# Three gemms of a two-block network take their product in token form, and the mixed value is turned by transposes

## Chip, cores and metric

The kernel runs on one core of a Trainium2 chip. The metric is the device time of one execution in microseconds, as the median of the runs. Engines: PE (TensorE, the matrix engine, with PEld for its weight loads), DVE (VectorE), ACT (ScalarE), POOL (GpSimd), SP (which here only starts DMAs). Each engine runs its instructions in order.

## The reference, cut to what matters

256 tokens, width 2048. Two layers of a first block, then a second block with two mixers (rwkv7 and MLA), whose outputs go through a branch matrix each and are mixed by gates.

```python
# first block, both layers l
proj = h @ w_in[l]
u, z_s, q, k, v, z_a = jnp.split(proj, splits, axis=-1)
...
y_a = diff_attention(q, k, v, lam, sub_g[l], lambda_init).reshape(bsz, s, ATTN_WIDTH)
y_a = y_a * jax.nn.silu(z_a)
y = jnp.concatenate([y_s, y_a.astype(y_s.dtype)], axis=-1) @ w_out[l]
x = x + gate[:, None, :] * y
...
# second block
u = rms_norm_2(h, pre_mix_norm[i])
z = u @ w_in[i]
z_rw, z_mla, z_gate = jnp.split(z, (RW_COLS, RW_COLS + MLA_COLS), axis=-1)
y_rw = rwkv7_mixer(z_rw, ...)
y_mla = mla_mixer(z_mla, ...)
g_rw, g_mla = jnp.split(jax.nn.sigmoid(z_gate), 2, axis=-1)
mix = (g_rw * (y_rw @ w_branch_rw[i]) + g_mla * (y_mla @ w_branch_mla[i])) @ w_out[i]
h = h + rms_norm_2(mix, post_mix_norm[i])
```

`z_a` (1024 columns per layer), `z_gate` (4096 columns) and the two branch matrices (1024 x 2048 each) are the gemms that the change touches.

## The kernel before

**Products.** Every gemm (`gemm`, L178) is a loop over blocks of 512 weight columns and, inside, over pairs of 128-row k-tiles. Each step is a *product* (`product`, L203): one DMA of 512 KB of fp32 weights into `wraw` (four buffers), a cast on ACT to `whi` (L213, three buffers), a subtraction on DVE to `wlo` (L214, three buffers), and three matmuls for each piece (activations hi x weights hi, lo x hi, hi x lo), summed in PSUM banks called `acc` (four; a block holds two). There are 802 products; they are numbered here from 0 in the order of their casts.

A product has two forms. In the **feature form** (`feat`, L221) a 128 x 128 piece of weights is loaded into PE and the 256 tokens move: 24 matmuls of 256 columns, and the result has features on the partitions. In the **token form** (L244 to L246) 128 tokens of the activations are loaded and 512 weight columns move: 12 matmuls of 512 columns, and the result has tokens on the partitions. After the last k-tile of a block `evac` reads the two banks.

**Side chains.** The small work (scans, attention, the chunked rwkv recurrence) is written as generators in lanes; after each product `step` (L123) advances the first of each lane, `rate` steps per product. `bank` hands out the four other PSUM banks. From this program a scheduler of the tile framework, by its own estimate of times, makes the fixed order of each engine's instructions, so the same steps may stand elsewhere when the neighbours change.

**Where the change lies.**
- `layer` (L901): z_s and z_a are two gemms in feature form (L960, L961); `ev_z` writes silu's numerator to DRAM as [128 features, 512], and `gated` (L867) in `diff_attention` fetches z_a per pair of heads (L874), transposes the attention output on PE (L879), multiplies by z_a from PSUM (L880), and splits into hi and lo (L101, L102).
- `mixers`: `gates` (L1732) makes two blocks of 8 products at a time; the evacuation multiplies by the token factors `R2` on DVE (`scaled`, L1101), takes Tanh on ACT (L1737) and writes to DRAM. The gates stand between `rk` and `vv` (inputs of the rwkv units), `mla_input(0)` and `mla_input(1)`, in this order in the program: unit 0's inputs, gates 0 and 1, `rk(1)`, gates 2, `vv(2)`, `rk(2)`, gates 3 and 4, `rk(3)`, unit 3 started, gates 5, `mla_input(0)`, gates 6, `mla_input(1)`, gates 7.
- The chain of a unit: `rw_keys` and `rw_parts`, then the masks on the products `rw_mt` (L1311 to L1315), four levels of a triangular inverse (`rw_in` on PE L1332 and L1341, ACT L1333, POOL L1335, DVE L1342 and L1343), the chunk recurrence (`rw_pn`, `rw_pq`, L1382 to L1412), and `rw_out` (norm by groups, L1429 to L1451).
- `mla_input` (L1456): sums of squares on ACT (L1469), a reciprocal root on DVE (L146 to L152), and `ml_x` (L1476), which reads the two `acc` banks last.
- `ev_b` (L1800): the two branch gemms (16 products each); the gate is fetched from DRAM, multiplied on DVE (L1808, L1810), added on POOL (L1811) and split into `oh` and `ol`, the input of `w_out_2`.

## Time and profile before

| what | us |
|---|---|
| median of 3 runs | 2899.38 |
| lowest, highest | 2898.35, 2900.8 |
| the profiled execution: time | 2900.31 |
| the profiled execution: span | 2898.5 |
| PE busy | 2806.3 (97%) |
| DVE busy | 1864.2 (64%) |
| ACT busy | 1360.7 (47%) |
| POOL busy | 495.5 (17%) |

The profile is of one execution. Its busy shares are means over stages that differ; the stages that matter here are z_a of layer 0 (257 to 305 us) and layer 1 (830 to 876), the gates with the rwkv units (about 1320 to 1740), and the branches (about 1790 to 1904). In a row of the costliest groups the columns are the busy time, the mean duration of one, and the idle time of the engine ahead of them with what ended it. Matmuls are pipelined: a duration of 284 ns is not the pace, which is read from starts.

### The profile page before, as it was taken

What the parts mean: (1) busy time and instruction counts of PE and PEld (TensorE: products, weight loads), DVE (VectorE), ACT (ScalarE), POOL (GpSimd) and SP (SyncE); (2) the same over time, 40 slices, a digit from 0 to 9 for tenths busy, and PEclk for the clock granted to TensorE, in tenths of its full rate; (3) what the DMA queues carried; (4) which work ended last, traced back from release to release, by engine and by line L of the source; (5) the groups of instructions that cost most, each with busy time, mean ns of one, the idle gap of its engine ahead of it and who ended that gap; (6) DMA issues with size and microseconds to landing.
All of it is one profiled execution on the core that took longest, in us unless ns stands there. A gap on an engine that the chain in (4) does not pass through costs nothing.

```text
span 2898.5 us, 57323 instructions
## 1 busy us (share of the span) xinstructions
PE 2806.3 (97%) x23206; PEld 2509.7 (87%) x23206; DVE 1864.2 (64%) x3346; ACT 1360.7 (47%) x2245; POOL 495.5 (17%) x627
## 2 busy tenths in 40 slices
PE   5899999999999999999999999999999999999998
PEld 2588766787997789999999888999999999999987
DVE  1467854656579557677876856666776767644465
ACT  2543454564434555553444444444555555533344
POOL 5300240243002402202110200012110101100020
PEclk7999999999999999999999999999999999999999
DMA  8977767776666655665444455566666666655565
GB/s 278 325 231 261 259 223 244 232 254 208 186 211 213 192 171 179 194 204 161 132 131 136 139 147 164 175 203 227 192 182 186 184 183 182 180 188 184 184 196 168
DMA packets 303045, 571.26 MB, mean 197 GB/s; under 512 B 31966, under 2 KB 68378, under 8 KB 302394
## 3 DMA queue, kind: packets, MB, share of 16 engines
q1 hardware_dynamic: 302457, 566.53, 62.8%
q8 instruction: 182, 2.98, 0.4%
q0 software_dynamic: 320, 1.05, 0.1%
q14 instruction: 86, 0.70, 0.1%
HBM read 546.53 MB, written 20.97 MB: 196 GB/s over the span
## 4 chain that ended last, share of the span: by engine, by line
PE 85%; DVE 7%; DMA 4%; issue 1%; ACT 1%; SPq 1%; POOL 1%; DVEq 0%; ACTq 0%; POOLq 0%
PE acc L221 60%; PE acc L244 4%; PE acc L245 4%; PE acc L246 4%; PE mod_rows L358 4%; DVE wlo L214 2%; DMA wada<-in_w_ada 1%; PE s5g L707 1%; DMA wraw<-in_w_in 1%; PE da_s L828 1%; PE s5y L769 0%; ACT whi L213 0%; PE rw_in L1341 0%; PE rw_pq L1382 0%; PE s5wT L668 0%
## 5 line engine op out<-in xcount | busy, mean ns | idle before, releaser
L214 DVE TENSOR_TENSOR wlo<-wraw,whi 128x1024 fp32r<-128x1024 f32 x802 | 1008.1, 1258 | 725.2 <-ACT whi L213 710.7
L213 ACT CAST whi<-wraw 128x1024 fp32r<-128x1024 f32 x802 | 833.3, 1040 | 1043.4 <-PE acc L221 755.1
L221 PE MATMUL acc<-ufh,whi 128*128 128x256 f32 x1408 | 391.4, 284 | 3.8 <-ACT ufh L485 3.8
L221 PE MATMUL acc<-ufl,whi 128*128 128x256 f32 x1408 | 388.8, 283 | 0.3 <-DVE ufl L486 0.3
L221 PE MATMUL acc<-ufh,wlo 128*128 128x256 f32 x1408 | 387.9, 284 | 0.0
L221 PEld LDWEIGHTS acc<-ufh,whi 128*128 128x128 f32 x1408 | 267.6, 193 | 4.3 <-ACT ufh L485 4.3
L221 PE MATMUL acc<-u2h,wlo 128*128 128x256 f32 x944 | 265.5, 287 | 5.0 <-DVE wlo L214 5.0
L221 PEld LDWEIGHTS acc<-ufl,whi 128*128 128x128 f32 x1408 | 266.3, 192 | 0.5 <-DVE ufl L486 0.5
L221 PE MATMUL acc<-u2h,whi 128*128 128x256 f32 x944 | 266.3, 288 | 0.0
L221 PEld LDWEIGHTS acc<-ufh,wlo 128*128 128x128 f32 x1408 | 265.9, 192 | 0.1
L221 PE MATMUL acc<-u2l,whi 128*128 128x256 f32 x944 | 264.8, 288 | 0.0
L221 PE MATMUL acc<-hh,whi 128*128 128x256 f32 x768 | 214.2, 291 | 6.5 <-ACT hh L480 3.3
L221 PE MATMUL acc<-hl,whi 128*128 128x256 f32 x768 | 208.9, 284 | 1.8 <-DVE hl L481 1.8
L221 PE MATMUL acc<-hh,wlo 128*128 128x256 f32 x768 | 210.3, 286 | 0.3 <-DVE wlo L214 0.3
L221 PEld LDWEIGHTS acc<-u2h,wlo 128*128 128x128 f32 x944 | 178.1, 191 | 7.4 <-DVE wlo L214 5.6
L221 PE MATMUL acc<-ffh,whi 128*128 128x256 f32 x640 | 181.1, 283 | 0.0
L221 PE MATMUL acc<-ffl,whi 128*128 128x256 f32 x640 | 181.1, 283 | 0.0
L221 PE MATMUL acc<-ffh,wlo 128*128 128x256 f32 x640 | 181.0, 283 | 0.0
L221 PEld LDWEIGHTS acc<-u2h,whi 128*128 128x128 f32 x944 | 178.3, 191 | 3.0 <-issue 1.0
L221 PEld LDWEIGHTS acc<-u2l,whi 128*128 128x128 f32 x944 | 178.1, 192 | 2.8 <-issue 1.0
L358 PE MATMUL mod_rows<-wada,v 128*32 128x512 f32 x768 | 150.0, 648 | 18.9 <-DMA wada<-in_w_ada 18.9
L221 PEld LDWEIGHTS acc<-hh,whi 128*128 128x128 f32 x768 | 145.0, 194 | 25.7 <-issue 11.5
(636 smaller groups left out, 6418.3 us busy)
## 6 DMA issues: line engine op xcount, KB each, us to landing
wraw<-in_w_in SPq DMA_DIRECT2D x288, 512.0 KB
wada<-in_w_ada SPq DMA_DIRECT2D x192, 512.0 KB
wraw<-in_w_up SPq DMA_DIRECT2D x176, 512.0 KB
wraw<-in_w_out SPq DMA_DIRECT2D x96, 512.0 KB
wraw<-in_w_down SPq DMA_DIRECT2D x88, 512.0 KB
wraw<-in_w_in SPq DMA_DIRECT2D x72, 256.0 KB
wraw<-in_w_glu SPq DMA_DIRECT2D x32, 512.0 KB
wraw<-in_w_ple_gate SPq DMA_DIRECT2D x28, 512.0 KB
```

The lines of the kernel that those rows point to most:

```text
L213: nc.scalar.copy(hi[:, :nk, :nw], raw[:, :nk, :nw])
L214: nc.vector.tensor_sub(lo[:, :nk, :nw], raw[:, :nk, :nw], hi[:, :nk, :nw])
L221: return nc.tensor.matmul(o, w[:, i, fs[f]], x[k0 + i], start=first, stop=stop, skip_group_check=True)
L244: nc.tensor.matmul(o, xh[k][:, tsl], hi[:, i, :nw], start=st, stop=False)
L245: nc.tensor.matmul(o, xh[k][:, tsl], lo[:, i, :nw], start=False, stop=False)
L246: mm = nc.tensor.matmul(o, xl[k][:, tsl], hi[:, i, :nw], start=False, stop=sp)
L358: nc.tensor.matmul(ps[o, :], self.v1["c"][:, k:k + 1].to_broadcast([128, 32]), raws[g // 2][:, g % 2, :], start=k == 0, stop=k == 15, tile ...
L707: nc.tensor.matmul(ps[:, p * 64:p * 64 + 64], wts[q][:, p, i, :], u4[:, P % 4, P // 4, :], start=True, stop=True)
L828: nc.tensor.matmul(sps[m][:, :n], qT[64 * m:64 * m + 64, h, t * 128:t * 128 + 128], kT[64 * m:64 * m + 64, h, :n], start=True, stop=True)
```

## The change

z_a, the gates and both branches go from the feature form to the token form (`True` becomes `False` in the calls of `gemm`). What follows from the other layout:
- z_a lies in DRAM as [tokens, 1024]; `gated` reads it with two DMAs of two heads each and multiplies on DVE ahead of the transposes (L877 after), and `gain_tile` (L483) makes hi and lo from PSUM.
- The gates' Tanh reads PSUM with a scale per partition (`half`, half of the token factors), so that `scaled` is not called.
- `ev_b` adds on DVE, and a new chain `turn` in lane 2 transposes the mixed value (four PE transposes into a bank, ACT and DVE from PSUM) for `w_out_2`: 32 transposes of 128 x 128.

```diff
...
             za = self.t2("za")
-            self.hold(nc.sync.dma_start(za[:], zd[p]))
+            for h in range(2):
+                self.hold(nc.sync.dma_start(za[:, h * 256:h * 256 + 256].rearrange("p (t e) -> p t e", t=2),
+                                            zd[:, (2 * p + h) * 128:(2 * p + h) * 128 + 128].rearrange("(t p) e -> p t e", t=2)))
+            nc.vector.tensor_mul(yk[:], yk[:], za[:])
             yield
...
                 nc.tensor.transpose(tps[:, a * 128:a * 128 + 128], yk[:, a * 128:a * 128 + 128], self.ident[:])
-            nc.vector.scalar_tensor_tensor(za[:], tps[:], sg, za[:], op0=ALU.mult, op1=ALU.mult)
             for a in range(2):
-                self.split(hs[2 * p + a], ls[2 * p + a], za[:, a * 256:a * 256 + 256])
+                self.gain_tile(hs[2 * p + a], ls[2 * p + a], tps[:, a * 256:a * 256 + 256], sg)
...
-        zd = self.dram.tile([2, 4, 128, 512], F32, name=f"z{l}")
-        def ev_z(which):
-            def ev(bi, pts):
-                for i in range(2):
-                    th, z = self.t2("th"), self.t2("z")
-                    nc.scalar.activation(th[:], pts[i][:], AF.Tanh, scale=0.5)
-                    nc.vector.scalar_tensor_tensor(z[:], th[:], 1.0, pts[i][:], op0=ALU.add, op1=ALU.mult)
-                    nc.sync.dma_start(zd[which, bi * 2 + i], z[:])
-            return ev
-        self.gemm(xh, xl, w, self.blocks(w, 1024, 2048), True, ev_z(0))
-        self.gemm(xh, xl, w, self.blocks(w, 5120, 6144), True, ev_z(1))
+        zd = self.dram.tile([4, 128, 512], F32, name=f"z{l}")
+        def ev_z(bi, pts):
+            for i in range(2):
+                th, z = self.t2("th"), self.t2("z")
+                nc.scalar.activation(th[:], pts[i][:], AF.Tanh, scale=0.5)
+                nc.vector.scalar_tensor_tensor(z[:], th[:], 1.0, pts[i][:], op0=ALU.add, op1=ALU.mult)
+                nc.sync.dma_start(zd[bi * 2 + i], z[:])
+        self.gemm(xh, xl, w, self.blocks(w, 1024, 2048), True, ev_z)
+        za = self.dram.tile([S, 1024], F32, name=f"za{l}")
+        def ev_za(bi, pts):
+            for t in range(2):
+                th, z = self.t2("th"), self.t2("z")
+                nc.scalar.activation(th[:], pts[t][:], AF.Tanh, scale=0.5)
+                nc.vector.scalar_tensor_tensor(z[:], th[:], 1.0, pts[t][:], op0=ALU.add, op1=ALU.mult)
+                nc.sync.dma_start(za[t * 128:t * 128 + 128, bi * 512:bi * 512 + 512], z[:])
+        self.gemm(xh, xl, w, self.blocks(w, 5120, 6144), False, ev_za)
...
         ah, al = self.feat_pair("ya", 8)
-        chain = self.start(self.diff_attention(qT, kT, v, nlam, sg[:, 0:1], zd[1], ah, al))
+        chain = self.start(self.diff_attention(qT, kT, v, nlam, sg[:, 0:1], za, ah, al))
...
         self.gemm(gh, gl, wg, self.blocks(wg, 0, 1024), True, ev_ga, rate=1.5)
-        self.hold(nc.sync.dma_start(zst[:].rearrange("p (k f) -> p k f", k=4), zd[0].rearrange("k p f -> p k f")), 4)
+        self.hold(nc.sync.dma_start(zst[:].rearrange("p (k f) -> p k f", k=4), zd[:].rearrange("k p f -> p k f")), 4)
         for k in range(8):
...
         self.rw_setup()
-        gd = self.dram.tile([16, 128, 512], F32, name="gd")
+        gd = self.dram.tile([S, 2 * D], F32, name="gd")
+        half = self.cs.tile([128, 2], F32, name="rv_half")
...
             def ev(bi, pts):
-                for i in range(2):
+                for t in range(2):
                     g = self.t2("gate")
-                    self.scaled(g[:], pts[i][:], self.R2)
-                    nc.scalar.activation(g[:], g[:], AF.Tanh, scale=0.5)
-                    nc.sync.dma_start(gd[bl[bi] * 2 + i], g[:])
-            self.gemm(xh, xl, w, [self.cols(w, 4448 + 512 * b) for b in bl], True, ev, rate=1.0)
+                    nc.scalar.activation(g[:], pts[t][:], AF.Tanh, scale=half[:, t:t + 1])
+                    nc.sync.dma_start(gd[t * 128:t * 128 + 128, bl[bi] * 512:bl[bi] * 512 + 512], g[:])
+            self.gemm(xh, xl, w, [self.cols(w, 4448 + 512 * b) for b in bl], False, ev, rate=1.0)
         at, vt = {}, {}
...
         last = []
+        nc.vector.tensor_scalar(half[:], self.r2, 0.5, None, op0=ALU.mult)
         rk(0)
...
             def ev(bi, pts):
-                for i in range(2):
-                    p = bi * 2 + i
+                for t in range(2):
                     g = self.t2("gate")
-                    self.hold(nc.sync.dma_start(g[:], gd[which * 8 + p]))
-                    m = self.xpair(mix, p)
+                    self.hold(nc.sync.dma_start(g[:], gd[t * 128:t * 128 + 128, which * D + bi * 512:which * D + bi * 512 + 512]))
+                    m = mix[t][:, bi * 512:bi * 512 + 512]
                     if which == 0:
-                        nc.vector.scalar_tensor_tensor(m, g[:], 1.0, pts[i][:], op0=ALU.add, op1=ALU.mult)
+                        nc.vector.scalar_tensor_tensor(m, g[:], 1.0, pts[t][:], op0=ALU.add, op1=ALU.mult)
                     else:
-                        nc.vector.scalar_tensor_tensor(g[:], g[:], 1.0, pts[i][:], op0=ALU.add, op1=ALU.mult)
-                        nc.gpsimd.tensor_add(m, m, g[:])
-                        for a in range(2):
-                            k, cs = 2 * p + a, slice(a * 256, a * 256 + 256)
-                            nc.scalar.mul(oh[k], m[:, cs], 0.5)
-                            nc.vector.scalar_tensor_tensor(ol[k], m[:, cs], 0.5, oh[k], op0=ALU.mult, op1=ALU.subtract)
+                        nc.vector.scalar_tensor_tensor(g[:], g[:], 1.0, pts[t][:], op0=ALU.add, op1=ALU.mult)
+                        nc.vector.tensor_add(m, m, g[:])
+                if which:
+                    turns.append(self.start(turn(bi), 2))
             return ev
+        def turn(bi):
+            for _ in range(2 if bi < 3 else 0):
+                yield
+            for i in range(2):
+                ps = self.bank("mixT")
+                for a in range(2):
+                    k = 4 * bi + 2 * i + a
+                    for t in range(2):
+                        o = a * 256 + t * 128
+                        nc.tensor.transpose(ps[:, o:o + 128], mix[t][:, k * 128:k * 128 + 128], self.ident[:])
+                for a in range(2):
+                    k = 4 * bi + 2 * i + a
+                    part = ps[:, a * 256:a * 256 + 256]
+                    nc.scalar.mul(oh[k], part, 0.5)
+                    nc.vector.scalar_tensor_tensor(ol[k], part, 0.5, oh[k], op0=ALU.mult, op1=ALU.subtract)
+                yield
+        turns = []
         for which, (a, b, n) in enumerate(((rh, rl, "w_branch_rw_2"), (mh, ml, "w_branch_mla_2"))):
...
                 self.finish(chain)
-            self.gemm(a, b, I[n][0], self.blocks(I[n][0], 0, D), True, ev_b(which), rate=1.25)
+            self.gemm(a, b, I[n][0], self.blocks(I[n][0], 0, D), False, ev_b(which), rate=1.25)
+        for c in turns[:3]:
+            self.finish(c)
         for k in range(8):
...
```

**Order on PE, unit 3's chain.** `rw_*` are the chain of rwkv's unit 3; L244 to L246 (`acc`) are products, here of the second block's inputs and gates. Before, around `rw_mt` of that unit (inside product 397):

```order
L246 MATMUL acc<-whi,u2l 128x512
L244 MATMUL acc<-whi,u2h 128x512
L1398 MATMUL rw_pn<-rw_SV,rw_BT 64x64 x4
L1412 MATMUL rw_pq<-rw_SV,rw_a 64x64 x3
L1304 MATMUL rw_mt<-rw_Q,rw_v 128x128 x8
L245 MATMUL acc<-wlo,u2h 128x512
L246 MATMUL acc<-whi,u2l 128x512
```

After, from the place behind the eight first `rw_mt` of that unit to the first matmul of product 408 (the first of `mla_input(1)`):

```order
L1406 MATMUL rw_pn<-rw_SV,rw_BT 64x64 x4
L1420 MATMUL rw_pq<-rw_SV,rw_a 64x64 x3
L1390 MATMUL rw_pq<-rw_SV,rw_Q 128x64 x4
L1398 MATMUL rw_pn<-rw_rp,rw_a 64x64
L1312 MATMUL rw_mt<-rw_Q,rw_v 128x128 x8
L1398 MATMUL rw_pn<-rw_rp,rw_a 64x64 x3
L1420 MATMUL rw_pq<-rw_SV,rw_a 64x64 x4
L1340 MATMUL rw_in<-rw_sm 32x32 x32
L1349 MATMUL rw_in<-rw_sm 32x32 x32
L1340 MATMUL rw_in<-rw_sm 32x32 x32
L1349 MATMUL rw_in<-rw_sm 32x32 x32
L244 MATMUL acc<-whi,u2h 128x512
```

What moved: before, the eight `rw_mt` stand between two matmuls of one product. After, product 407 is followed by `rw_pn` x4, `rw_bt` x8, `rw_pq` and `rw_mt` x8 and the rows shown, with no product between 407 and 408.

**Order on DVE, the same chain.** L1318, L1324 (before) and L1326, L1332 (after) are transposes of the masked pieces, L1429 ff. and L1437 ff. the norm of the unit's output, L214 the wlo of a product. Before (the two wlo are of products 403 and 404):

```order
L1318 STREAM_TRANSPOSE rw_sm<-rw_sm 128x256
L1324 STREAM_TRANSPOSE rw_sm<-rw_sm 128x256
L98 COPY rw_a<-rw_pq 64x2x64
L214 TENSOR_TENSOR wlo<-wraw,whi 128x1024
L1429 TENSOR_REDUCE gn_m<-rw_a 128x8
L1430 TENSOR_SCALAR gn_m<-gn_m 128x8
L1431 TENSOR_TENSOR rw_a<-rw_a,gn_m 128x512
L214 TENSOR_TENSOR wlo<-wraw,whi 128x1024
L1435 TENSOR_REDUCE gn_s<-rw_a 128x8
```

After:

```order
L1326 STREAM_TRANSPOSE rw_sm<-rw_sm 128x256
L98 COPY rw_SV<-rw_pn 64x2x64
L1332 STREAM_TRANSPOSE rw_sm<-rw_sm 128x256
L98 COPY rw_a<-rw_pq 64x2x64
L1437 TENSOR_REDUCE gn_m<-rw_a 128x8
L1438 TENSOR_SCALAR gn_m<-gn_m 128x8
L1439 TENSOR_TENSOR rw_a<-rw_a,gn_m 128x512
L1443 TENSOR_REDUCE gn_s<-rw_a 128x8
```

What moved: the wlo of products. After, these rows lie within 59 rows (from the copy of `rw_BT` to `ml_x` of `mla_input(0)`) behind the wlo of product 410, and the next wlo, of product 411, follows two rows behind them.

**Order on DVE, the gates' evacuation.** `gate` is a block of gates (here block 6), `yrl` the low part of unit 3's output. Before:

```order
L1451 TENSOR_TENSOR rw_a<-rw_a,gn_g 128x512
L1101 TENSOR_TENSOR gate<-acc,R_12939 128x512 x2
L102 TENSOR_TENSOR yrl<-rw_a,yrh 128x256 x2
L214 TENSOR_TENSOR wlo<-wraw,whi 128x1024
```

After, the same steps of the chain:

```order
L1351 STREAM_TRANSPOSE rw_sm<-rw_sm 128x256
L1459 TENSOR_TENSOR rw_a<-rw_a,gn_g 128x512
L214 TENSOR_TENSOR wlo<-wraw,whi 128x1024
L102 TENSOR_TENSOR yrl<-rw_a,yrh 128x256 x2
L214 TENSOR_TENSOR wlo<-wraw,whi 128x1024
```

What moved: L1101 is gone from DVE, and wlo (L214) stands between the chain's rows.

## Rows read from the trace of the kernel before

**Rows 1.** The page: totals (busy us, share, count); chain by line.

```profile
PE 2806.3 (97%) x23206; PEld 2509.7 (87%) x23206; DVE 1864.2 (64%) x3346; ACT 1360.7 (47%) x2245; POOL 495.5 (17%) x627
...
PE acc L221 60%; PE acc L244 4%; PE acc L245 4%; PE acc L246 4%; PE mod_rows L358 4%; DVE wlo L214 2%; DMA wada<-in_w_ada 1%; PE s5g L707 1%; DMA wraw<-in_w_in 1%; PE da_s L828 1%; PE s5y L769 0%; ACT whi L213 0%; PE rw_in L1341 0%; PE rw_pq L1382 0%; PE s5wT L668 0%
```

**Rows 2.** Windows: us; busy (count) of PE, PEld, DVE, ACT, POOL; PEclk; DMA.

```profile
257.00:305.00 48.00, 48.00 (x355) 39.26 (x353) 41.62 (x127) 14.17 (x15) 0.00 (x0) 1.00 0.86 283
...
830.00:876.00 46.00, 46.00 (x384) 43.70 (x380) 43.48 (x128) 16.68 (x19) 0.00 (x0) 1.00 0.81 257
876.00:930.00 54.00, 51.22 (x240) 37.34 (x240) 52.41 (x139) 22.64 (x34) 15.28 (x18) 0.97 0.72 227
1290.00:1322.00 32.00, 29.49 (x226) 28.42 (x225) 29.83 (x42) 17.82 (x28) 11.46 (x14) 0.95 0.51 146
...
1586.00:1625.00 39.00, 37.63 (x282) 33.33 (x281) 33.40 (x50) 20.84 (x34) 12.14 (x12) 1.00 0.45 132
1625.00:1740.00 115.00, 115.00 (x1342) 99.49 (x1341) 75.54 (x158) 47.48 (x80) 8.13 (x7) 1.00 0.53 146
1856.00:1902.00 46.00, 46.00 (x386) 46.00 (x385) 32.85 (x37) 21.04 (x29) 10.60 (x6) 1.00 0.69 223
```

**Rows 3.** Waits, 1290 to 1740: engine, line <- releaser: us, times, longest.

```profile
ACT whi L213 <- PE acc L221: 89.3, 60, 3.2
```

**Rows 4.** Timeline of PE: start, us, instruction.

```profile
909.32 0.87 PE L812 MATMUL toT<-ident,roped 128*128 128x128 f32 x6
909.95 0.47 PE L245 MATMUL acc<-wlo,hh 128*128 128x512 f32 x1
...
911.18 0.39 PE L245 MATMUL acc<-wlo,hh 128*128 128x512 f32 x1
...
917.55 0.39 PE L246 MATMUL acc<-whi,hl 128*128 128x512 f32 x1
```

**Rows 5.** Tiles za and gate: count, ns min/median/max, first and last start.

```profile
L874 SPq DMA_DIRECT2D za<-z x8: 326/361/557, 519.8 to 1132.3; - x8
L880 DVE SCALAR_TENSOR_TENSOR za<-da_t,sg,za x8: 737/748/751, 541.4 to 1152.9; 128x512 f32<-128x512 f32 x8
...
L1101 DVE TENSOR_TENSOR gate<-acc,R x16: 669/687/693, 1320.0 to 1739.0; 128x512 f32<-128x512 f32 x16
...
L1811 POOL TENSOR_TENSOR mix<-mix,gate x8: 1294/1789/2284, 1868.0 to 1903.8; 128x512 f32<-128x512 f32 x8
```

**Rows 6.** Windows of the stretch of unit 3; the second of L214 alone (DVE).

```profile
1630.54:1668.18 37.64, 37.64 (x518) 33.21 (x517) 30.36 (x75) 15.14 (x25) 5.54 (x5) 1.00 0.51 141
...
1630.54:1668.18 37.64, 11.09 (x10) 1.00 0.51 141
```

**Rows 7.** The page, costliest groups: busy us, mean ns, idle before.

```profile
L214 DVE TENSOR_TENSOR wlo<-wraw,whi 128x1024 fp32r<-128x1024 f32 x802 | 1008.1, 1258 | 725.2 <-ACT whi L213 710.7
L213 ACT CAST whi<-wraw 128x1024 fp32r<-128x1024 f32 x802 | 833.3, 1040 | 1043.4 <-PE acc L221 755.1
```

**Rows 8.** Groups by line, 1585 to 1745: busy us, mean ns, idle before.

```profile
L1321 POOL TENSOR_TENSOR rw_sm<-rw_sm,rwc 128x256 f32<-128x256 f32 x1 | 0.7, 742 | 35.0 <-DVE rw_sm L1311 35.0
...
L1469 ACT ACTIVATE ml_j<-acc 128x512 f32<-128x512 f32 x4 | 2.4, 600 | 1.1 <-PE acc L246 1.1
...
L1333 ACT COPY rw_sm<-rw_in 128x256 f32<-128x256 f32 x4 | 1.4, 362 | 2.0 <-PE rw_in L1332 2.0
...
L1433 ACT ACTIVATE rw_a<-rw_a 128x512 f32<-128x512 f32 x1 | 0.6, 636 | 1.0 <-DVE rw_a L1431 1.0
...
L1390 PE MATMUL rw_pn<-rw_rp,rw_a 64*64 64x64 f32 x56 | 4.7, 235 | 0.0
...
L1341 PE MATMUL rw_in<-rw_sm 32*32 32x32 f32 x256 | 3.2, 194 | 0.0
...
L1304 PE MATMUL rw_mt<-rw_Q,rw_v 64*128 64x128 f32 x32 | 2.3, 285 | 0.0
```

**Rows 9.** Timeline of DVE, one hand-over in the chain: start, us, wait.

```profile
1635.81 0.29 DVE L1405 TENSOR_TENSOR rw_st<-rw_pn,rw_st 128x128 f32<-128x128 f32 x1 [1.46 <-PE rw_pn L1398]
```

## The prediction

> **What bounds the kernel now.** I read four views in this order. First the totals and the chain that ended last: PE is busy for 97% of the span, and 60% of the chain are matmuls of L221, the form that this change removes in three places [rows 1]. So a shorter PE instruction stream is worth something, and idle PE time costs its full length. Second, the stretches in which the converted products lie [rows 2]: PE is busy all of 1625 to 1740 (the later gates) and of 1856 to 1902 (a branch), while DVE has room there (75.54 of 115 us; 32.85 of 46). In the second layer DVE is as full as PE: 43.48 of 46 us from 830 to 876, and 52.41 of 54 right after. Third, the waits: through the gates ACT's cast waits 60 times for PE to give a buffer back [rows 3], so the three-deep weight buffers are full and PE sets the pace. Fourth, the order in which the new program puts its instructions, since PE and DVE run in order and a shorter stream that stands still behind another engine gains nothing.
>
> **What a converted product saves.** A product is two k-tiles by 512 columns of weights: 24 matmuls of 256 moving columns before, 12 of 512 after. 1856 to 1902 is a stretch of nothing but the first kind: 46.00 us for 386 is 0.119 us each, about 0.120 with the few lost records [rows 2], so 24 are 2.88 us. The second kind starts at 911.18 and, 28 matmuls on, at 917.55 [rows 4]: 0.2275 each, 12 are 2.73 us. I take 0.15 us a product, and 128 products change: 19 us at the most.
>
> The Trainium skill, page "TensorE: Matmul & The Clock Gate", section "Wait — 56ns, not 53.3ns?", puts a fixed 2.5 ns on top of each warm matmul's columns. An estimate by its figure is 109 ns for 256 columns and 216 for 512, so 0.03 us a product and 4 us in all, which the new transposes would eat: by that page the conversion is worth nothing. The rows above disagree (120 and 227), and I go by the rows.
>
> **Part by part.**
> - *z_a, 16 products in each layer.* In layer 0 they lie in 257 to 305, where PE never rests and DVE is busy 41.62 of 48 us [rows 2]: 16 x 0.15 = -2.5 us. In layer 1 DVE fills up as soon as PE shortens, so I take half: -1.2 (0 to -2.5).
> - *z_a read by tokens.* In `gated` the multiply by z_a now stands ahead of the transposes and on DVE, and DVE waits for its DMA; queued behind it are the next products' wlo. The first read was issued at 519.8 and its first user ran at 541.4 [rows 5], 21 us, so the wait costs nothing; half-sized rows would have to be over 10 us later to be seen. DVE's work stays about the same: the pass over 512 columns at 748 ns [rows 5] becomes a multiply of that size, and the two subtractions behind it read PSUM instead. 0 (0 to +1).
> - *Gates, 64 products:* 64 x 0.15 = -10 us. The per-token factor goes into ACT's Tanh, so DVE loses 16 x 687 ns = 11 us [rows 5], which makes it unlikely that DVE becomes the bound on the way; PE's own waits here were small (1.4 us idle in 1586 to 1625) [rows 2]. I take -10 (-6 to -10).
> - *Branches, 16 products each:* -2.5 and -2.5 us. The add of L1811 leaves POOL (1.8 us each) [rows 5] for DVE, which has 13 us free in 1856 to 1902; its 8 instances cost nothing there. The 32 new transposes lie on PE: six in a row take 0.63 us (909.32 to 909.95) [rows 4], 0.105 each: +3.4. The last block's turn comes after its products, but the following gemm reads those tiles last. The branches come to -1.6 (-4 to +1).
>
> So far -15 us: -2.5, -1.2, -10, -1.6.
>
> **What the order adds.** The converted products carry the mixers' gates, and beside these runs rwkv's chain of four units. I number products by their casts, from 0. In the order before, unit 3's chain after its `rw_bt` copy is dealt out among products 395 to 407, and through it (1630.54 to 1668.18) PE is never idle: 37.64 of 37.64 us [rows 6]. In the new order this part of the chain stands in one block: after product 407 PE has 32 small matmuls and 128 of `rw_in` in a row and no product, and DVE has 59 rows without one wlo, between that of product 410 and that of 411. Among the last of the 59 are `ml_x`, which alone frees a bank that product 408 (the second `mla_input`) writes. PE cannot pass over it.
>
> How long PE stands: the wlo of 410 needs a whi cast into the buffer of 407, so both follow product 407: 1.0 + 1.2 us [rows 7]. Then the 59 rows of DVE. The trace of before has these very instructions from 1630.54 to 1668.18: DVE busy 30.36 us, of which wlo are 11.09 [rows 6]; 19.3 us remain. That is 21.5 us without a gap. In the chain DVE also waits, with nothing else left to do: for POOL's three products after the last mask (3 x 0.74), for `rw_in` and ACT's copy of it (0.36), for ACT's square (0.64) and its two sums of squares (2 x 0.6) [rows 8]; together 4.4 us if none overlaps, 25.9 in all. Of this PE works about 6 us, an estimate: 128 `rw_in` at 3.2/256, 16 `rw_mt` at 2.3/32 and 32 more at 4.7/56 [rows 8] are 5.5, and something for the changes between them. That work was there before. **Idle PE: 25.9 - 6 = +20 us.** Lower bound 21.5 - 6 = 15.5. Upper bound: the whole 37.64 us of before without the nine wlo that leave it, 37.64 - 10 = 28, plus the 2.2 ahead, less 6: 24.
>
> A second, smaller block stands after product 427, where the chain's last matmuls meet `mla_input`'s eight transposes: two round trips between PE and a copy more than before. From such trips in the trace (an `rw_pn` on PE, the copy, the add: 1.5 us of DVE's wait before L1405) [rows 9] I take +3 us (1 to 6).
>
> After an idle PE the granted clock has fallen before: in 1290 to 1322, with PE idle 2.5 us, it is 0.95 on average, in 876 to 930 it is 0.97 [rows 2]; either is 1.6 us of a full clock. One such dip more after the block: +1.6 (0 to 4).
>
> **The sum.** -15 + 20 + 3 + 1.6 = +9.6, on the profiled execution's 2900.3: 2910. That execution lies 0.9 above the median of the runs (2899.4), so the forecast is 2909 us, 0.3% slower.
>
> **Rivals.**
> 1. *The block is covered: faster, 2887.* If DVE runs much of its 59 rows before product 407 ends, PE finds `ml_x` done. Then the block costs 3 us or so: 2899.4 - 15 + 3 = 2887. For it: before, the same chain was wholly hidden [rows 6], and DVE is not full in 1625 to 1740. Against: the 59 rows begin behind the wlo of product 410, whose buffer product 407 still holds, and each round trip in them passes through PE rows that stand behind 407. It decides at 15 us of idle PE; below that the change is a gain. 0.18.
> 2. *The two sides cancel: no change, 2899.* The block at its lower bound (15.5), the second at 1, no clock loss: 2899.4 - 15 + 16.5 = 2901. 0.22.
> 3. *DVE-bound, and a longer block: 2920.* Gates gain 6 instead of 10, nothing in layer 1, the blocks 24 and 4, clock 3: 2899.4 - 10 + 31 = 2920. For it: in 1586 to 1625 DVE is busy 33.40 of 39 [rows 2], and unit starts bunch DVE work. 0.13.
> 4. *The two forms cost the same, and only the block is left: 2924.* The 0.120 of the old form would then come from what runs beside it, not from its form, and the converted products would take 2.9 us again: 2899.4 + 25 = 2924. The long even stretches at 0.120 speak against it [rows 2, 4]. 0.02. This is where the rule of the Trainium skill's page "TensorE: Matmul & The Clock Gate" (section "Wait — 56ns, not 53.3ns?"), given above, would lead.
>
> **How the numbers follow.** The forecast's own band (2905 to 2915) has 0.45, rival 2 0.22, rival 1 0.18, rivals 3 and 4 0.15. A measurement of this kernel can tell about 0.2% (5.8 us) from no change: faster is below 2893.6, slower above 2905.2. Rival 1 gives faster 0.18; rival 2 and a little of the forecast's lower edge give same 0.24; the rest, 0.58, is slower. The range reaches to the near part of rival 1 and all of rival 3: 2889 to 2920, leaving out some 0.1 at each end. Both signs have weight; the forecast's own range is 2905 to 2915.
>
> **What would show it.** Right: in the profile of the changed kernel a stretch near 1640 to 1680 with PE idle for 15 to 24 us in pieces, ended by DVE's `ml_x` (PE's wait at L244), POOL, ACT and DVE handing over to each other meanwhile, and a PEclk below 1 behind it; L244 to L246 at 0.227 us pitch in the gates; DVE busy some 10 us less in total; the POOL add gone. Wrong: no PE wait over 5 us there (rival 1); a pitch in the gates near 0.24, or ACT's cast no longer waiting for PE but PE for wlo (rival 3). What would refute the steps one by one: z_a's DVE multiply waiting for its DMA; the last turn holding up the gemm of w_out.

## The result and the profile after

The changed kernel takes 2933.85 us (median of 4 runs, 2932.23 to 2937.55), the kernel before in the same job 2899.85 (2898.35 to 2900.8): a ratio of 1.0117, 95% interval 1.0104 to 1.0130. It is slower, as forecast, but by 34 us and not by 9.6, and outside the range. The profiled execution took 2932.74 us, its span is 2930.9.

The page of the changed kernel, totals and chain (columns as in [rows 1]):

```profile
PE 2820.4 (96%) x21702; PEld 2436.4 (83%) x21702; DVE 1856.7 (63%) x3339; ACT 1365.0 (47%) x2245; POOL 481.3 (16%) x619
...
PE acc L221 49%; PE acc L245 8%; PE acc L244 8%; PE acc L246 8%; PE mod_rows L358 4%; DMA wada<-in_w_ada 2%; DVE wlo L214 1%; PE s5g L707 1%; PE da_s L828 1%; PE s5y L769 1%; ACT whi L213 0%; PE rw_pq L1390 0%; PE rw_in L1349 0%; PE da_w L861 0%; PE rw_mt L1312 0%
```

PE has 1504 rows fewer than before and is busy 14 us longer. Where the time came in is read from the ends of ACT's 802 casts (L213), the n-th of before against the n-th of after, in the two profiled executions:

| cast of product | before, us | after, us | difference | what lies in between |
|---|---|---|---|---|
| 56 | 326.2 | 324.7 | -1.5 | layer 0 up to z_a, half of q |
| 80 | 424.3 | 430.0 | +5.7 | rest of q, and k, of layer 0 |
| 320 | 1311.8 | 1318.8 | +7.0 | rest of both layers |
| 408 | 1670.7 | 1657.0 | -13.7 | rwkv units and gates |
| 416 | 1703.1 | 1718.4 | +15.3 | end of unit 3 |
| 432 | 1760.7 | 1785.0 | +24.3 | `mla_input`, last gates |
| 440 | 1789.3 | 1820.7 | +31.4 | start of MLA |
| 480 | 1926.9 | 1957.7 | +30.8 | MLA, branches |
| 801 | 2870.1 | 2900.8 | +30.7 | the rest |

Of the -1.5 at product 56, -0.5 is there at product 32, where z_a begins. So there are three places: 7 us that came in within 24 products of layer 0, a gain of 21 through the units (part of it chain work that is only put off), and 45 us given back between products 408 and 440. First the forecast block, in PE's timeline of the changed kernel (start, us, instruction, idle before it in brackets):

```profile
1663.08 0.40 PE L246 MATMUL acc<-whi,u2l 128*128 128x512 f32 x1
1663.41 0.45 PE L1398 MATMUL rw_pn<-rw_rp,rw_a 64*64 64x64 f32 x8
1663.79 1.09 PE L1299 MATMUL rw_bt<-ident,rw_v 128*128 128x128 f32 x8
1664.94 0.32 PE L1420 MATMUL rw_pq<-rw_SV,rw_a 64*64 64x64 f32 x2
1665.42 2.38 PE L1312 MATMUL rw_mt<-rw_Q,rw_v 64*128 64x128 f32 x16 [0.16 <-ACT rw_BT L96]
...
1671.97 1.97 PE L1390 MATMUL rw_pq<-rw_SV,rw_Q 128*128 128x64 f32 x8 [3.42 <-ACT rw_SV L96]
...
1681.38 0.69 PE L1420 MATMUL rw_pq<-rw_SV,rw_a 64*64 64x64 f32 x6 [2.96 <-DVE rw_SV L98]
...
1687.59 1.08 PE L1340 MATMUL rw_in<-rw_sm 32*32 32x32 f32 x64 [2.95 <-DVE rs_t L151]
...
1691.34 0.33 PE L1349 MATMUL rw_in<-rw_sm 32*32 32x32 f32 x9 [1.17 <-issue]
1691.60 0.80 PE L244 MATMUL acc<-whi,u2h 128*128 128x512 f32 x1
1692.19 0.63 PE L245 MATMUL acc<-wlo,u2h 128*128 128x512 f32 x1
1692.62 0.63 PE L246 MATMUL acc<-whi,u2l 128*128 128x512 f32 x1
```

Product 407 ends at 1663.4 and product 408 begins at 1691.60: 28.2 us in which PE runs only small rows of the chain and stands between them until ACT or DVE has copied the last result. In [rows 6] the same part of the chain cost PE no idle time. The first matmuls after it start every 0.43 us, where [rows 4] had 0.2275: of its two levels (1.2 and 2.4 GHz) TensorE is at the lower. The windows of the changed kernel (columns as in [rows 2]) show that, and that it happens twice more:

```profile
1650.00:1690.00 40.00, 28.44 (x411) 23.25 (x410) 26.03 (x68) 11.61 (x28) 3.62 (x5) 0.75 0.30 90
1690.00:1720.00 30.00, 28.83 (x376) 21.77 (x366) 15.80 (x30) 10.65 (x17) 2.03 (x2) 0.88 0.37 107
1720.00:1760.00 40.00, 40.00 (x302) 33.05 (x302) 22.88 (x48) 18.43 (x30) 0.00 (x0) 1.00 0.63 169
1760.00:1790.00 30.00, 27.00 (x182) 23.38 (x181) 17.50 (x34) 9.84 (x21) 4.83 (x4) 0.83 0.28 80
1790.00:1825.00 35.00, 31.26 (x148) 24.61 (x147) 20.65 (x43) 14.31 (x22) 1.29 (x1) 0.90 0.43 134
```

The granted clock is 0.75, 0.88, 0.83 and 0.90 in four of the five stretches; in the kernel before it is 1.00 from 1625 to 1740 [rows 2]. PE is idle 11.56 and 1.17 us in the first two, which is the block's 12.7 us of idle time, and 3.00 and 3.74 in the last two. In the second and third dip stand the chain's last links and the group norm's turn, here from PE's timeline:

```profile
1768.32 0.45 PE L1406 MATMUL rw_pn<-rw_SV,rw_BT 128*64 128x64 f32 x8 [1.10 <-DVE rw_SV L98]
...
1772.55 1.97 PE L1496 MATMUL ml_t<-ident,ml_x 128*128 128x128 f32 x8
...
1799.13 0.44 PE L1453 MATMUL gn_t<-ident,rw_a 128*128 128x128 f32 x2 [3.74 <-DVE rw_a L1445]
```

### The profile page after: what moved, and what is told of

The parts are those of the page before. It is cut to its first block, busy times and chain, and to the rows that moved or that the text cites. A ratio compares the mean times of both kernels' runs of the same rounds, so it can differ in the third digit from the quotient of the medians.

```text
span 2930.9 us, 54316 instructions
## 1 busy us (share of the span) xinstructions
PE 2820.4 (96%) x21702; PEld 2436.4 (83%) x21702; DVE 1856.7 (63%) x3339; ACT 1365.0 (47%) x2245; POOL 481.3 (16%) x619
## 4 chain that ended last, share of the span: by engine, by line
PE 87%; DVE 6%; DMA 4%; issue 1%; ACT 1%; SPq 1%; POOL 0%; DVEq 0%; ACTq 0%; POOLq 0%
PE acc L221 49%; PE acc L245 8%; PE acc L244 8%; PE acc L246 8%; PE mod_rows L358 4%; DMA wada<-in_w_ada 2%; DVE wlo L214 1%; PE s5g L707 1%; PE da_s L828 1%; PE s5y L769 1%; ACT whi L213 0%; PE rw_pq L1390 0%; PE rw_in L1349 0%; PE da_w L861 0%; PE rw_mt L1312 0%
## 5 line engine op out<-in xcount | busy, mean ns | idle before, releaser
L214 DVE TENSOR_TENSOR wlo<-wraw,whi 128x1024 fp32r<-128x1024 f32 x802 | 1008.8, 1259 | 757.3 <-ACT whi L213 747.0
L213 ACT CAST whi<-wraw 128x1024 fp32r<-128x1024 f32 x802 | 833.5, 1040 | 1051.3 <-PE acc L221 601.8
L245 PE MATMUL acc<-wlo,hh 128*128 128x512 f32 x512 | 204.8, 400 | 2.9 <-DVE wlo L214 2.9
L246 PE MATMUL acc<-whi,hl 128*128 128x512 f32 x512 | 202.1, 395 | 0.0
L244 PE MATMUL acc<-whi,hh 128*128 128x512 f32 x512 | 195.8, 400 | 0.0
L358 PE MATMUL mod_rows<-wada,v 128*32 128x512 f32 x768 | 160.7, 644 | 19.0 <-DMA wada<-in_w_ada 19.0
L221 PE MATMUL acc<-hh,whi 128*128 128x256 f32 x512 | 140.1, 292 | 6.5 <-ACT whi L213 3.8
L221 PE MATMUL acc<-hl,whi 128*128 128x256 f32 x512 | 136.9, 286 | 2.8 <-DVE hl L481 2.8
L221 PE MATMUL acc<-hh,wlo 128*128 128x256 f32 x512 | 138.5, 289 | 0.3 <-DVE wlo L214 0.3
L244 PEld LDWEIGHTS acc<-whi,hh 128*128 128x128 f32 x512 | 96.1, 189 | 43.6 <-issue 18.3
L245 PEld LDWEIGHTS acc<-wlo,hh 128*128 128x128 f32 x512 | 96.6, 189 | 41.9 <-issue 9.4
L245 PE MATMUL acc<-wlo,u2h 128*128 128x512 f32 x320 | 129.8, 406 | 1.4 <-DVE wlo L214 1.3
L246 PE MATMUL acc<-whi,u2l 128*128 128x512 f32 x320 | 128.2, 401 | 0.0
```

The source lines that it names most:

```text
L213: nc.scalar.copy(hi[:, :nk, :nw], raw[:, :nk, :nw])
L214: nc.vector.tensor_sub(lo[:, :nk, :nw], raw[:, :nk, :nw], hi[:, :nk, :nw])
L221: return nc.tensor.matmul(o, w[:, i, fs[f]], x[k0 + i], start=first, stop=stop, skip_group_check=True)
L244: nc.tensor.matmul(o, xh[k][:, tsl], hi[:, i, :nw], start=st, stop=False)
L245: nc.tensor.matmul(o, xh[k][:, tsl], lo[:, i, :nw], start=False, stop=False)
L246: mm = nc.tensor.matmul(o, xl[k][:, tsl], hi[:, i, :nw], start=False, stop=sp)
```

## The experiments

Each run is timed beside the kernel before on the same chip; the difference is between the medians. A *place in the order* is where the fixed order of an engine has an instruction, counted in products.

### One part alone

**e1_za**: only z_a in token form, with its read.

```diff
...
-        self.gemm(xh, xl, w, self.blocks(w, 5120, 6144), True, ev_z(1))
...
+        self.gemm(xh, xl, w, self.blocks(w, 5120, 6144), False, ev_za)
...
```

> Only z_a goes to the token form (with its store by tokens, the two reads and the multiply on DVE); gates and branches stay as before. Order theory (the loss sits where the new order breaks up or bunches the side work): the order of this kernel has 74 pairs of mod_rows and 40 fours instead of 53 and 51, as the changed kernel has, so the 7 us that the changed kernel had lost by product 320 come back in full, and all of it around products 60 to 72: 2907 us, with PE at L358 some 10 us longer. Rival (the new multiply on DVE waits for z_a): also some +7, but in the attention, with a wait of DVE for the za DMA. Form theory (the token form is dearer than counted, wherever it stands): a quarter of the changed products, a quarter of +34: 2908.

2911.90 against 2901.74: +10.2, ratio 1.0032 (1.0022 to 1.0043). The theories' times lie too close together to decide; the place does: 7.2 us come between the casts of products 56 and 80 (+0.4 to +7.6), PE is busy 10.0 us longer at L358 (below), and DVE's multiply waits 0.9 us in all, for POOL and not for the z_a transfer.

**e2_gates**: only the gates.

```diff
...
-            self.gemm(xh, xl, w, [self.cols(w, 4448 + 512 * b) for b in bl], True, ev, rate=1.0)
...
+            self.gemm(xh, xl, w, [self.cols(w, 4448 + 512 * b) for b in bl], False, ev, rate=1.0)
...
```

> Only the mixers' gates go to the token form; z_a and the branches stay in the feature form, so the branches read the gates in the wrong layout (the same bytes and row sizes) and the output is not the reference's. Order theory: the order shows the same long block after product 407 (160 small matmuls on PE, 59 rows on DVE) and the one after 427, so the loss of the changed kernel between products 320 and 440 comes back in full: 24 us, 2924. Form theory: half of the changed products, half of +34: 2917.

2925.99 against 2901.74: +24.3, ratio 1.0084 (1.0068 to 1.0101).

**e3_branches**: only the branches and the turn.

```diff
...
-            self.gemm(a, b, I[n][0], self.blocks(I[n][0], 0, D), True, ev_b(which), rate=1.25)
+            self.gemm(a, b, I[n][0], self.blocks(I[n][0], 0, D), False, ev_b(which), rate=1.25)
...
```

> Only the two branch gemms go to the token form, with the add on DVE and the turn by transposes; the gates stay in the feature form and are read in the wrong layout, so the output is not the reference's. Order theory: no block and no pair more in the order than before, 32 products at -0.15 us and 32 transposes at +0.105: -1.5 us, 2898. Form theory: a quarter of +34: 2908.

2901.35 against 2901.74: -0.4, ratio 0.9996 (0.9985 to 1.0007). The three add up to +34.0, the whole change: within the noise nothing comes from their meeting. The gates alone bring the blocks, and z_a alone brings the loss in the layers.

### The blocks: order or form

**e5_before_block**: the kernel before, in feature form; only the place of unit 3's rows on PE is moved behind product 407.

```diff
...
+        for i in self.late:
+            self.tc.add_manual_dep(i, self.hist[-1], mybir.DependencyInfo(
+                mybir.DependencyClass.NoSync, mybir.DependencyReason.DATA), reason="late")
...
```

> The kernel before, all in the feature form; alone the PE order of unit 3's chain is changed: what the program emits of it during mla_input(0) and gates(6) is put behind product 407's last matmul (order alone). The order then shows 60 rows of DVE without a wlo between products 410 and 411 and 160 small matmuls without a product after 407, as in the changed kernel; the blocks after 427 are not imposed. Order theory: PE stands about as long as in the changed kernel, 28 us from 407 to 408 of which 6 are its own work, and some 3 more are lost to a half clock: +22 to +25, 2925. Form theory (the longer feature products cover the chain): within 5 us of before, 2902 to 2907.

2925.42 against 2899.83: +25.6, ratio 1.0087 (1.0072 to 1.0102). The window of the block, and two of PE's waits in 1600 to 1960 (engine, line <- releaser: us, times, longest):

```profile
1660.00:1690.00 30.00, 20.23 (x380) 18.46 (x378) 20.81 (x59) 7.16 (x16) 3.68 (x5) 0.71 0.30 88
```
```profile
PE gn_t L1450 <- DVE rw_a L1442: 3.3, 1, 3.3
...
PE acc L249 <- DVE ml_x L1481: 1.7, 1, 1.7
```

No product was changed and the loss is there: the order makes it, not the token form. By the casts, 21 us come between products 404 and 412 (-4.0 to +17.2), the forecast block; some 4 of them are chain work that had stood ahead of 404 and is only put off, and from product 400 (-0.3) to 416 (+14.7) the loss is 15. Another 10 come between 428 and 444 (+16.6 to +26.5), where the changed kernel has its later dips. So those come in the old form too, once the chain is late.

**e4_paced** and **e6_paced6**: the changed kernel, with a bound on how far PE's order may let the chain fall behind its place in the program (3 products and 6).

```diff
...
             self.product(xh, xl, kt, k0, nk, nw, src, feat, pts[bi], before is not None and bi == 0 and k0 < 16)
+            if self.pace and len(self.marks) >= self.pace and self.marks[-self.pace]:
+                mine = next(i for i in nc.cur_bb.bb.instructions[n:] if i.engine == mybir.EngineType.PE)
+                self.tc.add_manual_dep(mine, self.marks[-self.pace], mybir.DependencyInfo(
+                    mybir.DependencyClass.NoSync, mybir.DependencyReason.DATA), reason="pace")
...
```

> The whole change, and the order on PE pinned in the second block's mixers: a product may not stand ahead of side matmuls that the program emitted three or more products earlier (order alone, no wait for a semaphore). The blocks after 407 and 427 are gone from the order, the pairs of mod_rows remain. Order theory: the blocks' cost goes: layers +7, gates 64 products at some -0.2 each, branches -1: 2893, with PE's waits in 1640 to 1810 under 5 us and PEclk 1.00 there. Form theory: PE then waits for the chain at the pinned places instead, and the time stays near the changed kernel's: 2930.

> The whole change with the same pin as in the paced run, but six products of slack instead of three: the chain stands at most 5 to 7 products behind the program, as in the kernel before (4 to 8), where the changed kernel lets it fall 17 behind. No block is left in the order; up to product 386 it is nearly the changed kernel's order, in which PE had no wait. Order theory: gates -14, layers +9 (mod_rows), branches 0: 2897. Rival (after the run with three): the chain is a row of hand-overs that the shorter products can't cover at any slack, and PE's waits only move: 2920 or more.

With 3: 2930.71 against 2901.74, +29.0, ratio 1.0103 (1.0085 to 1.0122). The number that the order theory gave (2893) failed, and that of its rival came (2930). With 6: 2911.45 against 2899.83, +11.6, ratio 1.0042 (1.0027 to 1.0057), between the two forecasts (2897, and 2920 or more). By the casts 6 of these 11.6 us are there by product 320, so even with 6 the second block gives nothing back. Windows of e4_paced, and the largest of PE's waits in 1290 to 1960, of e4_paced and then of e6_paced6:

```profile
1500.00:1550.00 50.00, 43.92 (x241) 33.42 (x241) 34.37 (x59) 20.81 (x37) 8.74 (x12) 0.90 0.41 116
...
1600.00:1650.00 50.00, 44.16 (x257) 33.97 (x253) 35.91 (x57) 24.34 (x43) 9.69 (x12) 0.86 0.40 117
1650.00:1700.00 50.00, 50.00 (x571) 38.72 (x565) 35.00 (x80) 18.78 (x31) 4.75 (x6) 1.00 0.45 127
```
```profile
PE rw_pn L1416 <- DVE rw_SV L99: 10.8, 3, 3.8
PE rw_pq L1400 <- ACT rw_SV L97: 7.4, 3, 2.5
```
```profile
PE rw_pn L1408 <- DVE rw_rp L99: 5.2, 5, 1.8
PE rw_pq L1430 <- DVE rw_SV L99: 3.8, 2, 1.9
```

The block is gone (PE is busy 50.00 of 50 in 1650 to 1700), but with 3 PE now stands in each unit where its order demands a link that ACT or DVE hasn't copied yet. A looser bound has fewer such waits. The chain is a row of hand-overs that needs its time: with 3 the order waits at each, and the changed kernel's order puts them all behind the last product that could cover them. The best slack between was not looked for.

**e9_own_pool**: the changed kernel, with buffers of their own for `mla_input`'s row statistics.

```diff
...
-            ss, rs = self.ty("ml_s", 2), self.ty("ml_r", 2)
+            ss, rs = self.tm("ml_s", 2), self.tm("ml_r", 2)
...
-            self.rsqrt(rs, ss, 1.0 / 512, EPS, 2)
+            self.rsqrt(rs, ss, 1.0 / 512, EPS, 2, self.tm)
...
```

> The changed kernel, in which mla_input's small row tiles (ml_s, ml_r and the two of their rsqrt) have four buffers of their own and no longer take turns with those of the group norm in rwkv's chain; nothing else is edited. In the built order no chain matmul stands in a block between products 407 and 408 any more; in its place stand 140 rows of the chain behind product 423 (rw_in, gn_t, gn_g, ml_t) and 45 behind product 427 (rw_pn, rw_pq, ml_t). Theory 'shared buffers': the block behind product 407 is there because the row statistics of the MLA input cannot start before rwkv's group norm has given its buffers back; with buffers of its own the 28 us stretch between products 407 and 408 falls to under 5 us, and what was standing moves on to the two later places, where it is work that is ready rather than hand-overs for the larger part: 2912 to 2925. Rival 'evacuation': product 408 waits for the accumulators of the gates in any case; the stretch stays, about 2934.

2916.38 against 2900.58: +15.8, ratio 1.0050 (1.0035 to 1.0065), as theory 'shared buffers' had it. Its windows, and the first use of `ml_s` on DVE for `mla_input(0)`, in the changed kernel and then in e9:

```profile
1650.00:1690.00 40.00, 40.00 (x247) 31.46 (x246) 29.54 (x62) 16.51 (x26) 1.48 (x2) 1.00 0.60 171
...
1720.00:1760.00 40.00, 33.99 (x503) 28.88 (x492) 18.84 (x41) 13.59 (x32) 1.99 (x2) 0.83 0.34 97
1760.00:1790.00 30.00, 25.90 (x155) 21.64 (x154) 21.60 (x46) 10.64 (x17) 4.83 (x4) 0.84 0.35 106
```
```profile
1687.89 0.15 DVE L1479 TENSOR_TENSOR ml_s<-ml_s,rv 128x2 f32<-128x2 f32 x1
```
```profile
1640.91 0.15 DVE L1483 TENSOR_TENSOR ml_s<-ml_s,rv 128x2 f32<-128x2 f32 x1
```

PE is full in 1650 to 1690, so product 408 was held by a shared ring of 16 small buffers: handed out in the program's order, it made `ml_s` of `mla_input` wait for the group norm of unit 3, and `ml_x`, which frees the bank, behind it. But the chain is as late as in the changed kernel, and 26 us come between the casts of products 416 and 432 (from -13.8 to +12.6 against before).

### The layers: steps of mod_rows broken in two

The first layers' loss has another cause. `mod_rows` (L358) makes four matmuls a step, each of 32 columns and each into another 32 partitions of a bank (`tile_position=(0, 32 * g)`: another group of PE's columns). PE's timeline, of the kernel before and then of the changed one (each of these fp32 matmuls shows as two rows, so x8 is a whole step and x4 half a step; the next row's start tells its price):

```profile
339.47 1.06 PE L358 MATMUL mod_rows<-wada,v 128*32 128x512 f32 x8
340.46 0.50 PE L245 MATMUL acc<-wlo,hh 128*128 128x512 f32 x1
```
```profile
346.43 1.05 PE L358 MATMUL mod_rows<-wada,v 128*32 128x512 f32 x4
347.41 0.50 PE L246 MATMUL acc<-whi,hl 128*128 128x512 f32 x1
...
385.15 1.06 PE L358 MATMUL mod_rows<-wada,v 128*32 128x512 f32 x8
386.14 0.50 PE L244 MATMUL acc<-whi,hh 128*128 128x512 f32 x1
```

A whole step costs PE 0.99 us and half a step 0.98. From 324 to 390 us the trace has 2 halves and 5 wholes before, 12 halves and 1 whole after: 6 rows more, 5.9 us. By starts, `mod_rows` takes 13.8 us between the casts of products 56 and 80 before and 19.7 after; that is 5.8 of the 7.2 us that the kernel loses there. The page's group of L358, of before, of e1_za and of e7_before_mods (below):

```profile
L358 PE MATMUL mod_rows<-wada,v 128*32 128x512 f32 x768 | 150.0, 648 | 18.9 <-DMA wada<-in_w_ada 18.9
```
```profile
L358 PE MATMUL mod_rows<-wada,v 128*32 128x512 f32 x768 | 160.0, 640 | 21.5 <-DMA wada<-in_w_ada 21.5
```
```profile
L358 PE MATMUL mod_rows<-wada,v 128*32 128x512 f32 x768 | 121.0, 656 | 39.9 <-DMA wada<-in_w_ada 36.5
```

The same 768 take 10.0 us more with z_a alone, which is what e1_za lost. The Trainium skill, page "TensorE: Matmul & The Clock Gate", section "Measured speedup vs the span model", says that tiles packed side by side share one matmul's time, plus some 4 ns a tile; the trace agrees (0.98 us for half, 0.99 for the whole).

**e7_before_mods**: the kernel before, with the first matmul of each step behind both weight loads of the step, so that the four stay together. **e8_paced6_mods**: the same in e6_paced6. **e10_before_late_mods**: as e7, but not in the steps at the very start. **e11_za_late_mods**: as e10, with z_a in token form.

```diff
...
+                if g == 0 and not early:
+                    self.after(mm, ld)
...
```

(e7 and e8 without `and not early`.)

> The kernel before, with one edit: the first matmul of each mod_rows group waits for both weight transfers of the group, so that the four matmuls (which use four column groups of PE) stay together: pairs in the order 53 -> 2, fours 51 -> 73. In the traces a run of a pair takes as long as one of a four (1.2 us from the matmul ahead to the one behind). Theory (a broken four costs a whole run more): 26 fours put together save 26 x 1.1 = 28 us if no transfer is waited for longer, 2874; bounds 2874 to 2892. Rival (the second transfer comes late and PE stands for it, the time of the pairs was cover): 2898 to 2905.

> The whole change, six products of slack and the fours kept together: pairs 74 -> 7. If both hold, the run before it less 33 x 1.1 = 36 us: 2861. If only the fours: 2934 - 36 = 2898. If only the pin: 2897.

e7: 2899.28 against 2899.83, ratio 0.9997 (0.9987 to 1.0007): the theory missed, the rival's band holds it. L358 fell to 121.0 us, but PE's wait for the weights rose from 18.9 to 36.5; by the casts 10 us are lost by product 16 and 15 gained between 32 and 112. e8: 2909.41, ratio 1.0025 (1.0013 to 1.0038), 2 us under e6: missed in the same way.

> The kernel before, in which the first mod_rows matmul of a step waits for both weight loads of its step (so that its four matmuls stand together, in four row groups of the array), but only in the steps behind layer 0's own norm; the ones at the very start stay as they were. In the built order the rows of two fall from 53 to 13 and those of four rise from 51 to 71. Theory 'pairs': a row of two costs PE as long as a row of four (118 us of mod_rows before, 101 where all were together); without the 10 us that PE lost at the start when the early ones waited too, it is 2884 to 2890. Rival 'loads': the steps are paced by their weight loads, PE loses in waits what it saves in rows: 2898 to 2902.

2888.67 against 2900.58: -11.9, ratio 0.9958 (0.9943 to 0.9973). With the start left alone the gain stays. (The four lie in column groups, not row groups as this expectation says.)

> The z_a products by tokens alone (as in e1_za), with the mod_rows steps held together as in e10_before_late_mods. In the built order rows of two fall from 74 to 19, rows of four rise from 40 to 65. Theory 'pairs': what the z_a products cost in e1_za (+10 us) was their shorter run on the other engines that broke 11 more steps of mod_rows into pairs; held together, z_a costs nothing against e10_before_late_mods or gains 1 to 4 us (2881 to 2890). Rival 'z_a itself': the token form of z_a or its reads cost the 10 us by something else, and it stands 8 to 12 us above e10_before_late_mods.

2896.17 against 2900.58: -4.4, ratio 0.9986 (0.9977 to 0.9996), and 7.5 above e10, outside the theory's band and just under the rival's 8 to 12. Against e10's casts e11 is 1.9 us ahead at product 56 and then loses 12.6 by product 176 (-1.9 to +10.7). By the starts L358 is 7.8 of these (1.0 in products 56 to 72, 2.9 in 104 to 128, 3.9 in 128 to 176), since with z_a shortened more halves are left even so (19 rows of two in the order, 13 in e10). Over the whole kernel L358 takes 143.4 us by starts in e10 and 153.1 in e11, 9.7 more, and the two profiled executions lie 9.1 apart (2885.26, 2894.37). So it is `mod_rows` again; why some 5 us more come by product 176 and go later is open.

### The best of both

**e12_paced_late_mods**: gates, branches and turn in token form, z_a as before, with the bound of e6 at 10 products, the buffers of e9 and the steps of e10.

> Gates and branches by tokens with the turn for w_out_2, as in the changed kernel; z_a left as before. The rwkv chain's matmuls are held in the order to at most 10 products behind their place in the program, mla_input has its row tiles to itself as in e9_own_pool, and the mod_rows steps stand together as in e10_before_late_mods. In the built order no block of the chain is left. Theory 'order': against e10_before_late_mods only the shorter gates products remain (64 x 0.23 us = 14.6 us less) and up to 8 us of new hand-over waits inside the units, as in e6_paced6: 2870 to 2882. Rival 'the chain fills the time': PE waits for the chain wherever it is put, and the shorter products give nothing: 2886 to 2895.

2888.72 against 2900.58: -11.9, ratio 0.9953 (0.9935 to 0.9970); no different from e10, and in the rival's band. It beats both kernels, but the gates add nothing to it. Their gain is there and is spent: from the starts of all PE rows in products 316 to 496, the products take 549.4 us in e10 and 537.7 in e12, 11.7 less (11 to 13 by where the bounds are put). Given back are the 32 transposes of `mixT` (2.8), `toT` (0.8), and the chain's own rows with the waits behind them: `rw_pq` 3.3, `gn_g` 1.6, `rw_in` 1.4, `rw_mt` 1.2. Together 11.1; all other rows are 1.3 us shorter. The largest of its waits in 1290 to 1960:

```profile
PE acc L259 <- DVE wlo L228: 3.7, 3, 3.1
PE gn_t L1461 <- DVE rw_a L1453: 3.3, 1, 3.3
PE rw_bt L1307 <- DVE rw_v L1283: 1.9, 1, 1.9
```

## Why the prediction was right and wrong

- *The form's price* (0.15 us a product): 11.7 us over the 96 products of gates and branches in e12, 0.122 each with the waits that stand in them. Near, and on the side of the rows. Rival 4 falls. An estimate by the figure of the Trainium skill, page "TensorE: Matmul & The Clock Gate", section "Wait — 56ns, not 53.3ns?", would give 0.03; the runs disagree.
- *z_a* (-3.7): **the first step that failed.** Its own products, which lie at 245 to 305 us in layer 0 of the kernel before and not only from 257 on, gained some 2 us there (-0.5 at the cast of product 32, -2.5 at 50; forecast -2.5), and z_a's read cost nothing, as forecast: the multiply L877 waited 0.9 us in all, for POOL. But the part came to +10.2 (e1), since the sum had only the converted products in it and not the `mod_rows` steps beside them, which the new order breaks in two (74 rows of two where there were 53). No term was made of it.
- *Gates* (-10) and *branches* (-1.6): near. At 0.122 the gates' 64 products give 7.8 us, inside the -6 to -10. The branches alone are -0.4, within their -4 to +1; the transposes took 2.8 us in e12 (3.4 forecast), and POOL has 14.2 us less, the eight adds. ACT's cast still waits for PE in the gates, as [rows 3] had it.
- *The block behind product 407* (25.9 us, of which 20 idle): right in place and kind, and right in size **by luck**. It is 28.2 us long, but PE is idle in it for only 12.7, less than the prediction's lower bound (15.5) and than its sign of being right (15 to 24). Two errors cancel. PE's own work was put at 6 us, because rows of the trace were taken for instructions: an fp32 matmul shows as two rows, so the 128 `rw_in` of the order are all 256 rows of [rows 8], 3.2 us and not 1.6. The block has 344 rows, which at their pace in the kernel before (by starts, 1585 to 1745) are 9.7 us. They took 5.8 more (28.2 - 12.7 - 9.7), of which 4.6 from the first long wait on, at the lower clock; product 408 lost another 2.4 to it (12 matmuls at 0.43 us). For that the sum had 1.6 us in all. Together some 21 us of loss, but from other parts than forecast. No wait of PE there ends on `ml_x`, which runs at 1691.86, as product 408 begins; they end on the chain's own rows on ACT and DVE. The ring of buffers behind it (e9) was not in the working. Rival 1 and its bound fall as well: idle time under 15 us, and still no gain.
- *The second block* (+3, at most 6): **the second step that failed.** By the casts products 424 to 440 lost 17 us (+14.3 to +31.4), some 3 of them rows of the chain that had stood earlier. The term had two round trips at full clock. What stood there was all of the chain that the first block had not finished, with the group norm's turn behind it (3.74 us of idle PE at 1799.13): 6.7 us idle, and much of the rest at the lower level. e5 has 10 us there in the old form.
- *The clock* (+1.6, one dip, at most 4): **the third step that failed.** There are three dips. By the granted clock of the windows TensorE is at its lower level for some 44 us (twice what each lacks to 1.00, times its length: 20, 7, 10 and 7), and what runs in them takes twice as long: eight `rw_pq` of L1390 take 1.97 us after a wait, and 1.00 in e9 at full clock (below).

The misses by part: z_a 13.9, gates with blocks and clock 9.7 (24.3 against 14.6), branches 1.2; together 24.8, about the 24.4 between +9.6 and +34. The sign was right, but z_a's loss, which no rival had, is a third of the whole. Rival 3 had the longer blocks, but made them of a full DVE, which the windows don't show (26.03 of 40 us in the block).

## What to carry to other kernels

When products get shorter, a side chain that advances by hand-overs between engines does not, as here: look in the new order by how many products each link has fallen behind, and price the whole tail of the chain, not only the first place where it stands alone. Removing one such place (e9) took 18 of the 34 us off and six products of slack (e6) 22, but both left waits elsewhere, and three products of slack (e4) took off only 5. When the price of a row comes from a trace, count rows with it: here an fp32 matmul is one instruction of the order and two rows of the trace. And look at every piece of work that lies between the changed products: a group of matmuls that share the array costs its full time for each part when the order splits it, and holding it together was worth as much here (12 us) as the shorter products of gates and branches (11.7).

## What was not expected of the hardware

A half step of `mod_rows` costs as much as a whole one (0.98 and 0.99 us). And the clock fell where PE was not idle for long at a time: in 1650 to 1690 it is busy 28.44 of 40 us, its idle time comes in pieces of up to 3.42 us, and the granted clock is 0.75. The eight matmuls that take 1.97 us at 1671.97 in the changed kernel, in the timeline of e9_own_pool, where PE was not idle ahead of them:

```profile
1661.16 1.00 PE L1394 MATMUL rw_pq<-rw_SV,rw_Q 128*128 128x64 f32 x8
```
